# A hybrid encoder step on one core: the last projection as a software pipeline in program order, with blocks of 2, 2, 2, 2, 2, 1

## The chip, the cores and the metric

The kernel runs on one core of a Trainium2 chip. The metric is the device time of one execution in microseconds; the time before is the median of three runs. Engines are named as in the profile: PE (matrix multiply), PEld (its weight loads), DVE (vector), ACT (scalar), POOL (GpSimd), SP (the queue that issues most DMAs).

## The reference, cut to what matters

One layer of a streaming encoder. Three mixers read one normalised input; their outputs go through one output projection and are added to the residual stream. Then follows the gated feed-forward block, whose last product is what the change is about:

```python
x = x + jnp.concatenate([o_a, o_b, o_c], axis=-1) @ w_out
h = _rms_norm(x, norm2_g)
x = x + (jax.nn.silu(h @ w_gate) * (h @ w_up)) @ w_down
```

There are 1024 prompt rows and 64 sample rows (1088 together), a model width of 1024 and a hidden width of 2816. Everything is float32.

## The kernel before, in words

**Precision.** Each float32 operand is split into a high part (rounded by ACT, `acopy`) and a low part (the rest, a DVE subtraction, `tt`). A product is three matmuls: high x high, high x low, low x high.

**Gate and up.** The hidden width is cut into 11 stripes of 256 (`kp`), and each has a gate unit and an up unit: 22 units `u`. Each unit is a 2 x 2 block product by a seven-product scheme (Winograd's form of Strassen's), for two column halves `c` of the rows (`NB` = 256 and 288 wide). So a unit has 14 steps of 12 matmuls; units 0 and 21 run the seven steps of `c` = 0 and then those of `c` = 1, the others alternate. The results of an up unit are multiplied into `gate[c, i, j]`, and the generator `hidden(kp, c)` forms the seven left operands that the down stage needs, splits them (ACT and DVE, through tiles `e` and `ds`) and writes them to `hd` in DRAM; the sample's rows go to `hs`. `hidden` runs in small pieces, one at each step of a later unit; that of the last unit runs inside the down stage.

**Down.** The 11 stripes are worked off in blocks, `KB`. For each block there are four pairs of row tiles (`PAIRS`), and each pair has seven products (`STEPS`). Each product is 3 matmuls per stripe into a bank Y, Z or X. After each product DVE adds the bank to a row tile (`y_add` into `yf`), and later products of the pair add onto the same bank: Y takes products 0, 2, 4 and 6, Z takes 1 and 5, X takes 3. So product 2 may only start when the accumulation after product 0 has read Y, and so on. The sample's rows need two steps more in each block (8 matmuls per stripe in all). In the last block an output goes out by `y_out` (a DMA on SP) after each of the products 3, 4, 5 and 6 of a pair.

**Weights of down.** For each stripe `d_prep` loads four blocks of 128 x 512 (DMAs from POOL's queue), forms the differences T1 to T4 on POOL (`G.tensor_tensor`), and splits eight blocks (ACT rounds, DVE subtracts). They live in slots of 128 x 512 (`DS`). The left operands `a` are loaded from `hd` by `a_load` (SP) into a ring of nine tiles; `fetch` loads the next wanted one at each step.

**What sets the order.** The lists `work` and `plans` give the order in which the code names the operations, and a planner with a cost model orders each engine's queue from it. In the down loop `prep(b + 1)` takes one piece of the next block's plan after each step where enough slots are free, and the rest at the block's end. A queue runs in order: an instruction that waits holds up all behind it on its engine.

Of the kernel before, what the change touches and what calls it, by code (L numbers as in the profile page):

```python
# [7 lines left out]
F32 = mybir.dt.float32  # L8
# [7 lines left out]

EPS = 1e-6
# [35 lines left out]
def hybrid_step(ctx, tc, x_prompt, x_sample, cache_k, cache_v, st_gdn, st_conv, norm1_g, w_in, conv_w, a_log,  # L53
# [1397 lines left out]
    ev, _ev = pool("ffne", "right")  # L1451
    xb, _xb = pool("hT1", "right")
    xb_.append(xb)
    later = []
# [116 lines left out]
    hid = []  # L1571
    xs1 = x_sums(1)
    w_loads(1)
    for u in range(22):
        sa, sb_ = unit_steps(u, 0), unit_steps(u, 1)
        steps = sa + sb_ if u in (0, 21) else [s for p in zip(sa, sb_) for s in p]
        for i, s in enumerate(steps):
            s()
            flush()
            for q in hid[:1] if u < 21 else ():  # L1580
                if next(q, 1):
                    hid.remove(q)
            if u == 0 and i < 7:
                next(xs1, None)
            if i >= 7 or u not in (0, 21):
                n = i - 7 if u in (0, 21) else i // 2
                if u in (0, 21) or i % 2:
                    WS.give(*WA[u].pop(PRODUCTS[n][0]))
            if i == 7 - (u > 0) and u + 1 < 22:
                w_sums(u + 1)  # L1590
            if i >= 7 and u + 1 < 22:
                for n in ([i - 8] if 7 < i else []) + ([6] if i == 13 else []) if u == 0 else [i - 7]:
                    w_split(u + 1, PRODUCTS[n][0])
        WA.pop(u)
        if u + 2 < 22:
            w_loads(u + 2)


    _xb.close()
    _fl.close()  # L1600
    _xr.close()
    _xa.close()
    dp, _dp = pool("ffnd", "left")
    KB = ((0, 1), (2, 3, 4), (5, 6), (7, 8), (9, 10))
# [3 lines left out]
    D = {}  # L1608
    yf = {}
    lasts = {}  # L1610

    def y_tile(t):
        yf[t] = sb(dp, [128, DM], "yf%d" % t)

    def y_load(t):
        r = 64 if t == 8 else 128
        SP.dma_start(out=yf[t][:r], in_=yd[128 * t:128 * t + r, :])

    def a_tile():
# [12 lines left out]

    def d_prep(kp):


        L = D[kp] = {}

        def load():
            for i in range(2):
                for j in range(2):  # L1640
                    n = "B%d%d" % (i + 1, j + 1)
                    L[n] = DS.take()
                    f0 = 256 * kp + 128 * i
                    G.dma_start(out=L[n], in_=w_down[0, f0:f0 + 128, 512 * j:512 * j + 512])  # L1644

        def minus(n, a, b):
            L[n] = DS.take()
            G.tensor_tensor(out=L[n], in0=L[a], in1=L[b], op=ALU.subtract)  # L1648

        def sums(*args):  # L1650
            for q in args:
                minus(*q)

        def split(n):
            v, h, lo = L[n], DS.take(F32R), DS.take(F32R)
            lasts["A"] = acopy(h, v)
            lasts["V"] = tt(lo, v, h.bitcast(F32), ALU.subtract)
            L[n] = (h, lo)
            DS.give(v)
# [5 lines left out]
    def d_plan(kps):  # L1665
        heads, splits = zip(*[d_prep(kp) for kp in kps])
        plan = [h[0] for h in heads]
        if kps == KB[0]:
            plan += [x for y in zip(*heads) for x in y][len(kps):] + [x for y in zip(*splits) for x in y]
        else:  # L1670
            for h, x in zip(heads, splits):
                plan += h[1:] + x
        return plan

    AL = {}

    def a_load(key):
        b, p, n = key
        kps = KB[b]
        c, q = PAIRS[p][:2]  # L1680
        v = head if key == (0, 0, 0) else a_tile()
        SP.dma_start(out=v[:, :2 * len(kps)].bitcast(F32), in_=hd[n, 2 * c + q, :, 2 * kps[0]:2 * kps[-1] + 2, :])
        AL[key] = v

    def s_load(b):
        kps = KB[b]
        v = sb(dp, [128, 6, 128], "sm", F32R, bufs=2)
        SP.dma_start(out=v[:, :2 * len(kps)].bitcast(F32),
                     in_=hs[2 * kps[0]:2 * kps[-1] + 2].rearrange("f p t -> p f t"))
        AL[b] = v  # L1690

    def y_add(t, h, ps, b):
        c = slice(512 * h, 512 * h + 512)
        tt(yf[t][:, c], ps, yf[t][:, c], ALU.add)
# [10 lines left out]
    def pair_steps(b, p):  # L1705
        kps, banks = KB[b], {}

        def step(n, bank, adds):
# [5 lines left out]
            for k, kp in enumerate(kps):  # L1714
                bh, bl = D[kp][RIGHT[n]]
                if p == 3:
                    D[kp].pop(RIGHT[n])
                    DS.give(bh, bl)
                for l, r in ((a[:, 2 * k], bh), (a[:, 2 * k], bl), (a[:, 2 * k + 1], bh)):
                    T.matmul(ps, l, r, start=fresh and m == 0, stop=m == 3 * len(kps) - 1,  # L1720
                             skip_group_check=not fresh)
                    m += 1

            def add():
                for i, j, done in adds:
                    t = PAIRS[p][2 + i]
                    y_add(t, j, ps, b)
# [6 lines left out]
    def sample_steps(b):  # L1734
        kps = KB[b]

        def step(j):
            ps, v = mmb(), AL[b]
            m, last = 0, 4 * len(kps) - 1
            for k, kp in enumerate(kps):  # L1740
                for i in range(2):
                    B = D[kp]["B%d%d" % (i + 1, j + 1)]
                    for w in B:
                        mm(ps, v[:, 2 * k + i], w, m == 0, m == last)
                        m += 1
                    if (i, j) == (0, 1):
                        DS.give(*B)

            def add():
                slot = DS.take()  # L1750
                tmp = slot[:64]
# [4 lines left out]
                DS.give(slot)  # L1756
# [7 lines left out]
    for b in range(len(KB)):  # L1764
        order = ["s", 0, 1, 2, 3] if b else [0, "s", 1, 2, 3]
        for p in order:
# [8 lines left out]
    def fetch():  # L1775
        if wants:
# [3 lines left out]
    plans = [d_plan(kps) for kps in KB]  # L1780

    def prep(b, n=1, room=6):

        while n and b < len(KB) and plans[b] and len(DS.free) >= plans[b][0][0] + room:
            plans[b].pop(0)[1]()
            n -= 1

    fetch()
    prep(0, 2)
    fetch()  # L1790
    fetch()
    for t in PAIRS[0][2:]:
        y_load(t)
    for _ in range(3):
        fetch()
    prep(0, 6)
    y_tile(8)
    y_load(8)
    for p in PAIRS[1:]:
        for t in p[2:]:  # L1800
            y_tile(t)
    prep(0, 10, 0)
    fetch()
    fetch()
    for i, (b, p, n, f) in enumerate(work):
        if b == 0 and p == 0:
            prep(0, 2, 0)
            if n in (1, 4):
                y_load(PAIRS[1][2 + n // 4])
        if b == 0 and p in (1, 2) and n in (1, 4):  # L1810
            y_load(PAIRS[p + 1][2 + n // 4])
        if p == "s":
            prep(b, 99, 0)
# [3 lines left out]
        if hid and i > 4:  # L1817
            with tc.issue_after(lasts["A"].ins), tc.issue_after(lasts["V"].ins):
                if next(hid[0], 1):
                    hid.pop(0)  # L1820
            if not hid:
                _ev.close()
                dq, _dq = pool("ffne2", "right")
                DS.more(dq, "f", 16)
# [36 lines left out]
```

## Time and profile before

| | |
|---|---|
| time before, median of 3 runs | 1377.42 us (1375.39 to 1378.45) |
| the profiled execution: time | 1375.35 us |
| its span, first to last instruction | 1373.6 us |
| mean granted clock of PE | 0.986 |
| PE busy | 1324.0 us (96%) |
| DVE busy | 989.2 us (72%) |
| ACT busy | 678.7 us (49%) |
| POOL busy | 185.5 us (14%) |

All times of the profile count from the start of the span. A row of a group reads: line, engine, operation, what it writes and from what, shape, count, then busy time and mean duration in ns, then idle time of the engine just before and what ended it. A row of the busy times by stretch reads: stretch, its length, then for PE, PEld, DVE, ACT and POOL the busy time with the count of instructions, then the granted clock of PE (1.00 is full), the share of the DMA engines and GB/s. A row of the chain of waits or of the timeline begins with the start and the duration in us. In a row of DMA issues the last number is the median time from issue to landing. Most small operations are recorded at the line of a helper: L85 is `acopy`, L91 is `tt`, L94 is `mm`; L1464 is the gate/up product, L1720 the down product, L1644 and L1648 the load and the difference in `d_prep`, L1682 `a_load`, L1699 `y_out`.

### The profile page before, as it was taken

Reading aid. Unit: us, or ns where it says so; the run is one execution under the profiler, and the core shown is the slowest. Engines: PE = TensorE matmul, PEld = TensorE weight load, DVE = VectorE, ACT = ScalarE, POOL = GpSimd, SP = SyncE. Lnnn points to the kernel's source line nnn. Section 1 sums busy time; section 2 is a strip of 40 time slices with the busy share of each in tenths; the row PEclk is TensorE's granted clock in tenths of the full one; section 3 lists DMA queues with packets and bytes.
Section 4 is the critical chain, followed back from the end, with each engine's and each line's share of the span. In section 5 each row is a group of like instructions: output and inputs, shape, how many; then the busy total and the mean of one; then the engine's idle time right before and its main releaser. Section 6 shows DMA issues by size and latency. Waiting matters only on the chain.

```text
span 1373.6 us, 26500 instructions
## 1 busy us (share of the span) xinstructions
PE 1324.0 (96%) x9922; PEld 1179.7 (86%) x9922; DVE 989.2 (72%) x2296; ACT 678.7 (49%) x1733; POOL 185.5 (14%) x274
## 2 busy tenths in 40 slices
PE   6999999999999999999999999999999988998898
PEld 6988888888878877778999999999999966776687
DVE  5887877867788775498776677666776498566854
ACT  7677376674566654557544555445554333121200
POOL 3100130101222200200000000000000435151400
PEclk9999999999999999998999999999999989999999
DMA  8432332223333262221443454434544689665566
GB/s 258 118 80 60 97 99 78 78 63 79 83 93 93 62 216 65 101 71 53 153 125 114 152 173 137 124 119 141 174 151 123 214 283 325 190 196 172 180 180 233
DMA packets 201314, 188.99 MB, mean 138 GB/s; under 512 B 13819, under 2 KB 170464, under 8 KB 201186
## 3 DMA queue, kind: packets, MB, share of 16 engines
q1 hardware_dynamic: 196018, 171.43, 41.4%
q0 software_dynamic: 5008, 15.77, 3.4%
q8 instruction: 78, 1.28, 0.4%
q14 instruction: 50, 0.41, 0.1%
q10 hardware_dynamic: 160, 0.10, 0.0%
HBM read 135.72 MB, written 51.61 MB: 136 GB/s over the span
## 4 chain that ended last, share of the span: by engine, by line
PE 84%; DVE 7%; DMA 3%; issue 2%; ACT 2%; POOL 1%; SPq 0%; DVEq 0%; ACTq 0%; POOLq 0%
PE ax L1464 29%; PE mm L94 26%; PE ax L1720 10%; PE ax L94 10%; PE mm L1464 5%; DVE d L91 2%; PE mm L1720 2%; DVE yf L91 1%; DMA d<-in_ffn_w_down_dram 1%; PE ax L502 1%; PE ax L274 1%; DVE lw L91 1%; PE ax L837 1%; DVE f L91 1%; DMA xs<-in_x_prompt_dram 0%
## 5 line engine op out<-in xcount | busy, mean ns | idle before, releaser
L1464 PE MATMUL ax<-x,w 128*128 128x256 f32 (+1 forms) x2552 | 359.3, 288 | 0.0
L1464 PEld LDWEIGHTS ax<-x,w 128*128 128x128 f32 x2552 | 335.4, 191 | 0.2
L91 DVE TENSOR_TENSOR w<-w,w 128x512 fp32r<-128x512 f32 (+1 forms) x242 | 164.5, 688 | 87.8 <-PE ax L1464 51.3
L1720 PE MATMUL ax<-d,a 128*128 128x512 f32 x644 | 176.5, 406 | 19.1 <-DVE yf L91 15.5
L1720 PEld LDWEIGHTS ax<-d,a 128*128 128x128 f32 x644 | 124.9, 195 | 52.0 <-DVE yf L91 19.7
L94 PE MATMUL mm<-xh,hw 128*128 128x384 f32 (+1 forms) x432 | 151.3, 350 | 0.0
L94 PE MATMUL mm<-xl,hw 128*128 128x384 f32 (+1 forms) x432 | 143.6, 332 | 0.0
L94 PE MATMUL mm<-xh,lw 128*128 128x384 f32 (+1 forms) x432 | 143.2, 331 | 0.0
L85 ACT ACTIVATE hw<-wr 128x512 fp32r<-128x512 f32 (+2 forms) x168 | 99.7, 619 | 65.6 <-PE mm L94 55.1
L91 DVE TENSOR_TENSOR lw<-wr,hw 128x512 fp32r<-128x512 f32 (+2 forms) x168 | 110.8, 674 | 25.0 <-ACT hw L85 24.3
L91 DVE TENSOR_TENSOR yf<-ax,yf 128x512 f32<-128x512 f32 x120 | 82.2, 687 | 61.4 <-PE ax L1720 58.3
L1464 PE MATMUL ax<-xr,w 128*128 128x288 f32 x616 | 116.0, 296 | 0.0
L85 ACT ACTIVATE w<-w 128x512 fp32r<-128x512 f32 x154 | 94.5, 623 | 29.1 <-PE mm L1464 15.2
L85 ACT ACTIVATE s<-ax 128x256 f32<-128x256 f32 (+1 forms) x132 | 52.0, 394 | 87.8 <-PE ax L1464 87.5
L1464 PEld LDWEIGHTS ax<-xr,w 128*128 128x128 f32 x616 | 95.0, 188 | 0.2 <-ACT s L85 0.2
L94 PEld LDWEIGHTS mm<-xh,hw 128*128 128x128 f32 x432 | 81.1, 188 | 10.2 <-issue 7.3
L1644 POOL DMA_DIRECT2D d<-in_ffn_w_down_dram x37 | 19.8, 541 | 479.6 <-PE ax L1464 455.8
L94 PEld LDWEIGHTS mm<-xl,hw 128*128 128x128 f32 x432 | 81.4, 189 | 1.3 <-issue 0.7
L94 PEld LDWEIGHTS mm<-xh,lw 128*128 128x128 f32 x432 | 81.1, 188 | 1.2 <-issue 0.3
L85 ACT ACTIVATE d<-d 128x512 fp32r<-128x512 f32 x58 | 33.6, 622 | 75.2 <-POOL d L1648 47.9
L1464 PE MATMUL mm<-x,w 128*128 128x256 f32 (+1 forms) x528 | 70.6, 289 | 0.0
L88 DVE SCALAR_TENSOR_TENSOR tr<-tr,cw 128x384 f32<-128x384 f32 (+1 forms) x108 | 64.1, 594 | 7.2 <-ACT tr L85 6.2
(337 smaller groups left out, 2518.2 us busy)
## 6 DMA issues: line engine op xcount, KB each, us to landing
hd<-e SPq DMA_DIRECT2D x154, 256.0 KB, 2.4
wr<-in_w_in_dram SPq DMA_DIRECT2D x72, 512.0 KB, 3.9
a<-hd SPq DMA_DIRECT2D x112, 256.0 KB, 3.2
w<-in_ffn_w_gate_dram SPq DMA_DIRECT2D x44, 256.0 KB, 3.4
w<-in_ffn_w_up_dram SPq DMA_DIRECT2D x44, 256.0 KB, 3.5
a<-hd SPq DMA_DIRECT2D x28, 384.0 KB, 3.2
d<-in_ffn_w_down_dram POOLq DMA_DIRECT2D x37, 256.0 KB, 6.0
wr<-in_w_out_dram SPq DMA_DIRECT2D x9, 512.0 KB, 4.4
```

The costliest lines, as they stand in the source:

```text
L85: return A.activation(out=out, in_=in_, func=AF.Copy, scale=scale)
L88: return V.scalar_tensor_tensor(out=out, in0=in0, scalar=s, in1=in1, op0=op0, op1=op1)
L91: return V.tensor_tensor(out=out, in0=in0, in1=in1, op=op)
L94: return T.matmul(out, lhsT, rhs, start=start, stop=stop)
L274: T.transpose(b[k // 4][:, (k % 4) * r:(k % 4) * r + r], x[:r, k * 128:k * 128 + 128], ident[:r, :r])
L502: T.transpose(b[u // 4][:, (u % 4) * 128:(u % 4) * 128 + 128], src(u).rearrange("p h i -> p (h i)"), ident)
L837: T.transpose(PTp[0:r0 + cnt, j, kv, :], P[:, kv, 128 * j:128 * j + r0 + cnt], ident)
L1464: T.matmul(ps[:, :NB[c]], a[:, k, :], b[:, k, :], start=first and i == 0, stop=i == 11, skip_group_check=not first)
L1644: G.dma_start(out=L[n], in_=w_down[0, f0:f0 + 128, 512 * j:512 * j + 512])
L1720: T.matmul(ps, l, r, start=fresh and m == 0, stop=m == 3 * len(kps) - 1, skip_group_check=not fresh)
```

## The change

From unit 21 to the end the planner is switched off: on all five engines the instructions run in the order in which the code names them. The preparation of each block's weights is written out as a table of steps (`ORDER0` for block 0, within unit 21; `ORDER` for a later block, within the block before it). The blocks are (0,1), (2,3), (4,5), (6,7), (8,9), (10) where they were (0,1), (2,3,4), (5,6), (7,8), (9,10).

The weights are loaded as two rows of blocks per stripe, each 128 x 1024 (R1, R2), from SP's queue and no longer from POOL's. ACT and DVE split R1 and R2 in single operations of 1024; the differences are rounded and subtracted in pairs of 512 (T13, T24). The slots for them (`PT`) come from the places of the gate/up stage's right operands as each is used up (`left_over`): 15 and then 19, 2 more from `yf` places, and 8 where `hidden`'s tiles were, once `hidden` has ended. The differences, the tiles `a` and the sample's temporary share the 20 slots `w` of the gate/up weights (`WS`). `fetch` no longer uses a ring of nine but holds back when `AL` has nine entries. Within a step of the down loop the order is: the matmuls, the accumulation (and `y_out`), `fetch`, a load of `yf`, one piece of `hidden` on every second step, and up to three pieces of the next block's plan.

The diff, cut to its core:

```diff
+ENGINES = {getattr(mybir.EngineType, n) for n in ("PE", "DVE", "Activation", "Pool", "SP")}
...
+    KB = ((0, 1), (2, 3), (4, 5), (6, 7), (8, 9), (10,))
...
+        def load(i):
+            L["R%d" % (i + 1)] = t = PT.take()
+            f0 = 256 * kp + 128 * i
+            SP.dma_start(out=t.rearrange("p j c -> p (j c)"), in_=w_down[0, f0:f0 + 128, :])
...
+            G.tensor_tensor(out=block(t), in0=a, in1=b, op=ALU.subtract)
...
+        def rnd(n):
+            h = PT.take(F32R)
+            L[n, "h"] = h
+            if n[0] == "R":
+                acopy(h, L[n])
+            else:
+                for j in range(2):
+                    acopy(h[:, j], block(L["T" + n[1 + j]]))
+
+        def sub(n):
+            h, lo = L[n, "h"], PT.take(F32R)
+            L[n, "l"] = lo
+            if n[0] == "R":
+                tt(lo, L[n], h.bitcast(F32), ALU.subtract)
+                used(n)
...
+                for j in range(2):
+                    tt(lo[:, j], block(L[names[j]]), h[:, j].bitcast(F32), ALU.subtract)
+                    WS.give(L[names[j]])
...
+    ORDER0 = ((0, "aL1 aL2"), (1, "bL1 bL2"), (5, "aT1d aR1r"), (6, "bT1d aR1s bR1r"), (7, "aT3d bR1s"),
+              (8, "bT3d aR2r"), (9, "aT2d aT13r aR2s"), (10, "bT2d aT13s bT13r"), (11, "aT4d bT13s bR2r"),
+              (12, "bT4d aT24r bR2s"), (13, "aT24s bT24r"), (14, "bT24s"))
+    ORDER = ((0, "aL1 aL2"), (8, "aT1d aR1r"), (9, "aT3d"), (10, "aT2d aR1s"), (11, "aT4d aR2r"),
+             (12, "bL1 bL2 aT13r"), (13, "aR2s"), (14, "aT13s aT24r"), (16, "aT24s"), (19, "bT1d"), (20, "bT3d bR1r"),
+             (21, "bT2d"), (22, "bT4d bR1s bR2r"), (24, "bR2s bT13r"), (26, "bT13s bT24r"), (28, "bT24s"))
...
+    def prep(b, t, most=3):
+
+        while most and b < len(KB) and plans[b] and plans[b][0][0] <= t and len(PT.free) >= plans[b][0][1]:
+            plans[b].pop(0)[2]()
+            most -= 1
...
+    def s_load(b):
+        kps = KB[b]
+        AL[b] = v = WS.take(F32R)
...
+            ps, a = banks[bank], AL.pop((b, p, n))
...
+                for i, j, done in adds:
+                    t = PAIRS[p][2 + i]
+                    y_add(t, j, ps)
+                    if done and b + 1 == len(KB):
+                        y_out(t, j)
...
+        def step(j):
+            ps, v = mmb(), AL[b]
...
+    def fetch():
+        if wants and len(AL) < 9:
+            k = wants.pop(0)
+            s_load(k) if isinstance(k, int) else a_load(k)
...
     for u in range(22):
+        if u == 21:
+            ctx.enter_context(tc.manual_schedule(engines=ENGINES))
...
+            if u == 21:
+                left_over(i)
+                prep(0, i, 4)
+                if i > 7:
+                    fetch()
...
+    for i, (b, p, n, f) in enumerate(work):
+        if i and b > work[i - 1][0]:
+            start = i
+            prep(b, 99, 99)
+        f()
+        flush()
+        fetch()
+        if b == 0 and p in (0, 1) and n in (2, 5):
+            y_load(PAIRS[p + 2][2 + n // 5])
+        if hid and i > 1 and i % 2 == 0:
+            if next(hid[0], 1):
+                hid.pop(0)
+            if not hid:
+                _ev.close()
+                dq, _dq = pool("ffne2", "right")
+                PT.add(dq, "f", 8, 8)
+        prep(b + 1, i - start)
...
-    KB = ((0, 1), (2, 3, 4), (5, 6), (7, 8), (9, 10))
...
-                    G.dma_start(out=L[n], in_=w_down[0, f0:f0 + 128, 512 * j:512 * j + 512])
...
-        return ([(4, load), (2, lambda: sums(("T1", "B12", "B11"), ("T2", "B22", "T1"))),
-                 (2, lambda: sums(("T3", "B22", "B12"), ("T4", "B21", "T2")))],
-                [(2, lambda n=n: split(n)) for n in ("B11", "T1", "T2", "B21", "T3", "B22", "T4", "B12")])
...
-        if not (b == 0 and p in (0, "s")):
-            prep(b + 1)
-        if i + 1 < len(work) and work[i + 1][0] > b:
-            prep(b + 1, 99, 0)
```

In the tables `a` and `b` are the two stripes of a block, L1 and L2 their loads, T..d a difference on POOL, ..r a rounding on ACT, ..s a subtraction on DVE; the number is the step from which it may stand.

More of the change, by code (lines that the diff above doesn't have):

```diff
@@ new lines, in hybrid_step @@
+    work = []
+    for b in range(len(KB)):
+        for p in (["s", 0, 1, 2, 3] if b else [0, "s", 1, 2, 3]):
+            work += [(b, p, None, f) for f in sample_steps(b)] if p == "s" else \
+                    [(b, p, x[0], f) for x, f in zip(STEPS, pair_steps(b, p))]
+    wants = []
+    for b, p, n, f in work:
+        k = b if p == "s" else (b, p, n)
+        if k not in wants:
+            wants.append(k)
+    def fetch():
+        if wants and len(AL) < 9:
+            k = wants.pop(0)
+            s_load(k) if isinstance(k, int) else a_load(k)
@@ L1685, in s_load @@
[L1685 to L1694, printed above, removed]
-    def y_out(t, h):
-        c = slice(512 * h, 512 * h + 512)
-        dst = y_p[0, 128 * t:128 * t + 128, c] if t < 8 else y_s[0, :, c]
-        SP.dma_start(out=dst, in_=yf[t][:dst.shape[0], c])
@@ L1702, in hybrid_step @@
-    STEPS = ((0, "Y", ((0, 0, 0),)), (1, "Z", ((1, 1, 0),)), (2, "Y", ((0, 1, 0),)), (3, "X", ((0, 0, 1),)),
-             (4, "Y", ((1, 1, 1),)), (5, "Z", ((0, 1, 1),)), (6, "Y", ((1, 0, 1),)))
-    def pair_steps(b, p):
-        kps, banks = KB[b], {}
-        def step(n, bank, adds):
-            fresh = bank not in banks
-            if fresh:
-                banks[bank] = mmb() if bank == "X" else ax()
-            ps, a = banks[bank], AL.pop((b, p, n))
-            m = 0
[L1714 to L1727, printed above, removed]
-                    if done and b + 1 == len(KB):
-                        y_out(t, j)
-            later.append(add)
-        return [lambda x=x: step(*x) for x in STEPS]
@@ L1734, in sample_steps @@
[L1734 to L1751, printed above, removed]
-                c = slice(512 * j, 512 * j + 512)
-                acopy(tmp, ps[64:128, :])
-                tt(yf[8][:64, c], ps[0:64, :], yf[8][:64, c], ALU.add)
-                tt(yf[8][:64, c], tmp, yf[8][:64, c], ALU.add)
-                DS.give(slot)
-                if b + 1 == len(KB):
-                    y_out(8, j)
-            later.append(add)
-        return [lambda j=j: step(j) for j in range(2)]
@@ L1780, in hybrid_step @@
[L1780 to L1813, printed above, removed]
-        f()
-        flush()
-        fetch()
[L1817 to L1824, printed above, removed]
-        if not (b == 0 and p in (0, "s")):
-            prep(b + 1)
-        if i + 1 < len(work) and work[i + 1][0] > b:
-            prep(b + 1, 99, 0)
```

215 lines of the change are left out of this document (138 added, 77 removed).

## The prediction

> **What bounds the kernel now.** I read the page first: the span, the busy shares, the granted clock.
>
> ```profile
> span 1373.6 us, 26500 instructions
> PE 1324.0 (96%) x9922; PEld 1179.7 (86%) x9922; DVE 989.2 (72%) x2296; ACT 678.7 (49%) x1733; POOL 185.5 (14%) x274
> ```
>
> PE bounds the program, but the change touches only its last fifth. So next come the busy times by stretch, cut where PE stops being full; the fields are length, then busy time and instructions of PE, weight loads, DVE, ACT, POOL, then granted clock.
>
> ```profile
> 1074.80:1096.00 21.20, 21.20 (x170) 21.20 (x169) 6.54 (x13) 4.59 (x10) 12.89 (x15) 1.00 0.74 240
> 1096.00:1120.00 24.00, 17.72 (x53) 13.32 (x52) 22.91 (x33) 9.61 (x22) 13.08 (x18) 0.72 0.83 283
> 1120.00:1180.00 60.00, 50.96 (x205) 39.41 (x205) 51.46 (x83) 23.39 (x45) 22.70 (x21) 0.94 0.89 291
> 1180.00:1220.00 40.00, 40.00 (x175) 32.56 (x174) 16.51 (x22) 3.39 (x7) 6.08 (x5) 1.00 0.63 179
> 1220.00:1250.00 30.00, 22.81 (x89) 17.59 (x88) 27.15 (x36) 11.19 (x20) 17.20 (x15) 0.89 0.51 153
> 1270.00:1300.00 30.00, 25.90 (x110) 19.96 (x109) 25.64 (x36) 10.20 (x18) 14.26 (x13) 1.00 0.57 176
> 1300.00:1369.60 69.60, 69.60 (x303) 56.30 (x301) 35.49 (x52) 1.19 (x2) 0.00 (x0) 1.00 0.69 211
> ```
>
> The last gate/up unit (u = 21: 14 steps of 12 matmuls) fills 1074.8 to 1096.0 with DVE at 31% and ACT at 22%. The down stage runs from 1096.0 to 1369.6. The chain of waits gives its pace where nothing disturbs it:
>
> ```profile
> 1355.80 8.28 PE ax L1720 x36
> 1364.07 1.39 PE mm L1720 x6
> 1369.63 0.69 DVE yf L91
> ```
>
> One pair of seven products is 42 matmuls in 9.67 us, 0.230 us each. The code issues per 256 weight rows 4 pairs x 7 products x 3 and 8 for the sample, 92; times 11 is 1012, so PE needs 233.0 us, the same before and after. The stage takes 273.6, so 40.6 us are lost. By counts against 0.230: 11.8 in 1096-1120, 12.8 in 1120-1180, 9.5 in 1220-1250, 4.7 in 1270-1300. These are the stretches in which DVE is 86 to 95% busy. The list of waits, from 1050 on, says so:
>
> ```profile
> PE ax L1720 <- DVE yf L91: 20.6, 11, 3.5
> ```
>
> PE waits for DVE's accumulation into `yf`, which stands in DVE's queue behind bunches of weight subtractions. That is what the change spreads out.
>
> **The change part by part.** The groups of DVE and POOL from 1096 on, and ACT's from the page:
>
> ```profile
> L91 DVE TENSOR_TENSOR yf<-ax,yf 128x512 f32<-128x512 f32 x120 | 82.2, 687 | 61.4 <-PE ax L1720 58.3 <-DMA yf<-yd 2.6
> L91 DVE TENSOR_TENSOR d<-d,d 128x512 fp32r<-128x512 f32 x49 | 39.3, 840 | 1.8 <-ACT d L85 1.8
> L91 DVE TENSOR_TENSOR e<-g,e 128x256 fp32r<-128x256 f32 x10 | 4.4, 444 | 1.3 <-ACT e L85 1.3
> L1648 POOL TENSOR_TENSOR d<-d,d 128x512 f32<-128x512 f32 x18 | 27.3, 1530 | 11.2 <-DVE yf L91 6.0 <-PE ax L1720 3.2 <-DMA d<-in_ffn_w_down_dram 1.2
> L85 ACT ACTIVATE d<-d 128x512 fp32r<-128x512 f32 x58 | 33.6, 622 | 75.2 <-POOL d L1648 47.9
> ```
>
> When DVE has a backlog, 512-wide operations follow each other at 0.60 us (chain of waits):
>
> ```profile
> 1240.32 0.60 DVE d L91
> 1240.92 1.21 DVE yf L91 x2
> ```
>
> *Loads.* 44 loads of 256 KB leave POOL (44 x 0.54 = 24 us of a mostly idle engine, worth nothing on the path) and 22 of 512 KB go to SP. The nearest rows bound the landing at 3.2 and 4.4 us:
>
> ```profile
> a<-hd SPq DMA_DIRECT2D x112, 256.0 KB, 3.2
> d<-in_ffn_w_down_dram POOLq DMA_DIRECT2D x37, 256.0 KB, 6.0
> wr<-in_w_out_dram SPq DMA_DIRECT2D x9, 512.0 KB, 4.4
> ```
>
> I take 4.4 (same size and queue). Block 0's four go out by step 1 of u = 21 (1077.8), land by about 1083, and PE needs them at 1096: nothing, with 13 us of cover; without it, 4.4.
>
> *Block 0's preparation inside u = 21* is what can be gained at the start. ACT has 8 roundings of 1024 (8 x 1.24) in steps 5 to 13: it fits. DVE in order has 8 subtractions of 1024, at most 2 x 0.60 each, among the combines. The combine of step 10 starts at 1091.5; from there DVE owes seven combine operations (about 3.0) and five subtractions (5.9), so the last (`bT24s`) ends near 1100.4, and the first accumulation, queued behind it, near 1101.1. Product 2 writes the bank that this accumulation reads, and would start at 1098.8: PE loses 2.4.
>
> *Block 0 itself.* DVE still owes the last unit's `hidden` (about 9 us: 22 operations of 256 at 0.44 or less), 28 accumulations, 2.7 for the sample, 9.3 for block 1's subtractions: some 40 us against 42.5 of PE. Walking the order: `hidden` takes every second step up to 16, bL2 has no slot until `hidden` is done at step 16, and three subtractions then come in steps 16 and 17. An accumulation may be late by 0.7 us (the spare of a 1.38 us step); behind steps 8, 10 and 17 it is later, and PE waits 0.6, 0.8 and 2.8: 4.2. DVE beside POOL is the unknown:
>
> ```profile
> 1109.20 4.10 DVE L91 TENSOR_TENSOR ds<-g 128x256 f32<-128x256 f32 x1
> 1109.28 3.73 POOL L1648 TENSOR_TENSOR d<-d,d 128x512 f32<-128x512 f32 x3
> ```
>
> A 0.42 us operation lasted 4.10 beside three of POOL's. Bounds for the sixteen POOL subtractions near u = 21 and block 0: none hit, 0; all sixteen block for 1.53, 24. The mean subtraction of the stage, 840 ns, is 0.24 over its 0.60, so I am near the low end: 16 x 0.16 = 2.5. With 1 us for a clock drop, the start and block 0 cost 10.1 (bounds 6 to 32).
>
> *Blocks 1 to 4.* A block's 28 accumulations, sample and 8 subtractions are about 32 us of DVE in 42.5, one subtraction at a time, so a late accumulation mostly stays inside its 0.7 us. I take 3 in all (0 to 6) where before 14.2 were lost in 1220-1250 and 1270-1300.
>
> *One more block* adds 28 accumulations and 4 sample adds, about 22 us of DVE, and 29 loads of 0.32 on SP. They hide in the slack, except in block 5, where a product is 3 matmuls, 0.69, no more than its accumulation.
>
> *The last block's queue order* is what the change adds. `fetch` holds back at nine entries in `AL`, and the sample tiles are never taken out of `AL`: in block 5 six of nine are such, and only three products are loaded ahead (nine before). SP issues in program order, and each `y_out` waits for its accumulation. SP before, in its last stretch:
>
> ```profile
> 1355.83 0.32 SPq L1682 DMA_DIRECT2D a<-hd  x1
> 1356.55 0.34 SPq L1699 DMA_DIRECT2D out_dram<-yf  x1
> 1358.15 12.54 SPq L1699 DMA_DIRECT2D out_dram<-yf  x7
> ```
> ```profile
> SPq L1699 <- DVE yf L91: 16.4, 17, 5.1
> ```
>
> So `y_out` really stops SP (17 times). Now the load of product n + 3 stands right behind the `y_out` of product n, for n = 3 to 6. Landing of `a`, before and after stores join it (1331-1338, 1338-1345):
>
> ```profile
> L1682 SPq DMA_DIRECT2D a<-hd x5: 319/320/412, 1332.3 to 1337.9; - x5
> DMA to landing us min/median/max: 2.7/2.9/3.0
> ```
> ```profile
> DMA to landing us min/median/max: 3.8/3.8/3.9
> ```
>
> The new tiles are half as large; I take 2.9 (2.4 to 3.8). From the end of product 3: accumulation 0.03 + 0.69, store issue 0.03 + 0.34, landing 2.9, wake-up 0.1 = 4.09, while products 4 and 5 last 1.38: PE idles 2.71 before product 6. The same comes before product 2 of the next pair, behind the `y_out` of product 6. That is 4 + 3 gaps, 19.0. At the block's start the sample's stores hold product 3's load in the same way: DVE ends the sample's four adds 1.85 after the second sample product, + 0.03 + 0.34 + 2.9 + 0.1 = 5.2 against 2.1 us of products 0 to 2: 3.1. Sum 22.1 (18.6 to 28.8 by the landing).
>
> *Sum.* 1096.0 + 233.0 + 10.1 + 3 + 22.1 + 4.0 (from PE's end to the end of the span, as now: 1373.6 - 1369.6) = 1368.2, 5.4 less than 1373.6. The profiled execution took 1375.35, 2.07 under the median of 1377.42; I move by the same amount, to 1372.0.
>
> *Clock.* Gaps of 2.7 us are where the clock may drop. Two PE rows with their gap, and the stretches after:
>
> ```profile
> 1113.95 2.50 PE L1720 MATMUL ax<-d,a 128*128 128x512 f32 x5 [2.73 <-DVE yf L91]
> 1172.73 0.50 PE L1720 MATMUL ax<-d,a 128*128 128x512 f32 x1 [2.96 <-DVE yf L91]
> ```
> ```profile
> 1114.00:1116.00 2.00, 2.00 (x5) 1.62 (x6) 1.83 (x5) 0.05 (x1) 0.00 (x0) 0.50 1.03 404
> 1172.00:1174.00 2.00, 1.27 (x6) 1.05 (x7) 0.93 (x3) 1.72 (x4) 1.21 (x1) 1.00 0.39 144
> ```
>
> One gap of 2.73 left the clock at half, one of 2.96 did not. At half, a product of the last block takes 1.28; walking a pair as above gives 12.0 us instead of 10.25, so 7.0 more. The Trainium skill ("TensorE: Matmul & The Clock Gate", section "Why this matters for your kernels") puts the limit at gaps of about 3 us; by that rule the last block stays at full clock and the sum is as above, but the row at 1113.95 speaks against it.
>
> **The rivals.**
> A. *Half clock through the last block*: 1372.0 + 7.0 = 1379.0. For it the gap at 1113.95, and seven gaps in 40 us; against it the one at 1172.73.
> B. *The stores don't hold SP in effect* (loads run far enough ahead, or land in time): the last block loses only 3 by the accumulation chain, 1372.0 - 19.1 = 1352.9. Against it: 16.4 us of SP's waits on exactly these stores; for it: the 20 `w` slots would allow more than three tiles ahead.
> C. *Slower, by one mechanism: POOL blocks DVE in u = 21 and block 0.* There DVE has no slack, and each block of 1.53 goes straight to PE. The row of 4.10 speaks for it, the mean of 840 ns against it. All sixteen: 2.5 becomes 24, 1393; ten: 1385. It decides from 8.2 us more, about seven of the sixteen. The Trainium skill ("SBUF — State Buffer", section "Who interferes with whom") says that a DVE instruction with two SBUF inputs and a GpSimd instruction that reads SBUF exclude each other for a whole instruction; the trace agrees in that one row.
>
> **How the numbers follow.** 0.2% (2.75 us) is about what this measurement can tell from no change. My case 0.42 (1372.0, own range 1365 to 1379: of it 0.30 faster, 0.10 same, 0.02 slower), A 0.20 (0.04, 0.10, 0.06), B 0.18 (all faster), C 0.20 (0.02 same, 0.18 slower). Faster 0.52, same 0.22, slower 0.26. The range runs from B's 1353 to C's ten blocks, 1385.
>
> **What would show it.** PE at 0.230 per matmul at full clock without gaps over 1 us in blocks 1 to 4; a gap of 2 to 3 us at the third product of the down stage, led by DVE; in the last 45 us about seven gaps near 2.7, released by landings of `a`, with SP's `y_out` waiting on DVE just before. I am wrong if the last block has no such gaps (B), if its clock is 0.5 (A), or if DVE's subtractions before 1140 last over 2 us (C).

## The result, and the profile after

The changed kernel takes 1391.15 us, the median of four runs (1390.07 to 1394.69), beside 1376.72 for the kernel before on the same chip: a ratio of 1.0109, 95% interval 1.0086 to 1.0131. It is slower by 1.1%; 1372.0 had been predicted, with a range up to 1385. The profiled execution has this span and these busy times:

```profile
span 1389.8 us, 26486 instructions
PE 1326.8 (95%) x9922; PEld 1176.0 (85%) x9922; DVE 999.0 (72%) x2306; ACT 676.7 (49%) x1713; POOL 163.3 (12%) x230
```

PE's work is the same 9922 matmuls: of the 16.2 us by which the span grew, 13.4 are idle time of PE, and 2.8 are longer busy time for the same work. The busy times by stretch of the changed kernel, in the columns used before, say where:

```profile
1096.00:1120.00 24.00, 18.52 (x86) 14.78 (x84) 20.33 (x35) 4.64 (x11) 5.72 (x4) 1.00 0.89 308
1120.00:1180.00 60.00, 42.97 (x174) 33.45 (x175) 39.48 (x61) 17.38 (x33) 12.36 (x8) 0.89 0.80 260
1220.00:1250.00 30.00, 29.65 (x128) 23.54 (x127) 22.13 (x30) 4.32 (x6) 5.37 (x4) 1.00 0.52 164
1270.00:1300.00 30.00, 29.96 (x130) 23.70 (x129) 23.98 (x33) 3.85 (x6) 8.04 (x7) 1.00 0.50 162
1339.80:1386.00 46.20, 30.33 (x93) 19.02 (x91) 21.83 (x32) 1.19 (x2) 0.00 (x0) 0.85 0.52 162
```

The middle is what the change set out to make: PE is busy for 29.65 and 29.96 of 30 us in the two stretches where the kernel before had 22.81 and 25.90. The ends are worse: 42.97 of 60 us (50.96 before) in 1120-1180, and 30.33 of 46.2 us in the last block, where the kernel before ran its last 69.6 us without a gap. The list of waits of PE from 1050 on names DVE's accumulations first and landings of the left operands second:

```profile
PE ax L1721 <- DVE x L92: 20.0, 7, 12.3
PE ax L1721 <- DMA w<-hd: 12.4, 10, 2.3
PE ax L1721 <- issue: 4.2, 2, 2.5
```

(In this trace the row tiles `yf` carry the name `x`, the left operands `a` the name `w`, and the weights `x`, `xr` or `f`, after the pools their places come from. L86 is `acopy`, L92 `tt`, L95 `mm`; L1721 is the down product, L1682 `a_load`, L1703 `y_out`, L1627 a difference on POOL.)

I cut the stage at the first sample matmul of each later block, with which that block begins. The first of block 1 and of block 5:

```profile
1165.91 0.39 PE L95 MATMUL mm<-xr,w 128*128 128x512 f32 x1
...
1339.77 0.39 PE L95 MATMUL mm<-f,w 128*128 128x512 f32 x1
```

At 0.230 us a matmul, the start and block 0 (184 matmuls, 42.4 us) should take PE from 1096.0 to 1138.4; block 1 begins at 1165.9, so **27.5 us** are lost there. PE is idle for 22.4 of them: 0.93 before the last step of unit 21, and 21.5 from the stage's first product on. About 3 go because matmuls after the gaps run at a lower clock. And 1.9 were lost before the part that the change is about, since unit 21 began later in this execution than in the one profiled before (first row: before; second: changed; the variants below lie between 1074.9 and 1076.4):

```profile
1074.80 4.47 PE L1464 MATMUL ax<-x,w 128*128 128x256 f32 x36
```
```profile
1076.66 4.48 PE L1465 MATMUL ax<-x,w 128*128 128x256 f32 x36
```

Blocks 1 to 4 take 173.9 for 169.5: **4.4** lost. Block 5 takes 46.2 for 21.4: **24.8** lost. The kernel before lost 24.6 in 1096-1180, 14.2 in the middle and next to nothing at the end. So the middle gained 9.8 us, the last block lost some 24, and the start, where 14.5 were to be gained, lost 2.9 more.

**The last block.** Its PE rows with a gap over 1.8 us, and SP's rows around one of them:

```profile
1351.97 0.77 PE L1721 MATMUL ax<-x,w 128*128 128x512 f32 x1 [2.26 <-DMA w<-hd]
1363.67 0.47 PE L1721 MATMUL ax<-x,w 128*128 128x512 f32 x1 [2.24 <-DMA w<-hd]
1374.29 0.47 PE L1721 MATMUL ax<-x,w 128*128 128x512 f32 x1 [1.97 <-DMA w<-hd]
1385.11 0.47 PE L1721 MATMUL ax<-x,w 128*128 128x512 f32 x1 [2.24 <-DMA w<-hd]
```
```profile
1354.77 1.82 SPq L1682 DMA_DIRECT2D w<-hd  x4
1360.43 0.34 SPq L1703 DMA_DIRECT2D out_dram<-x  x1
1360.86 0.38 SPq L1682 DMA_DIRECT2D w<-hd  x1
```

SP issues four loads by 1356.6, then nothing until the store of 1360.43, whose accumulation has just ended; the load behind it, issued at 1360.86, lands just before PE resumes at 1363.67. A pair comes round every 11.0 us ((1385.11 - 1351.97) / 3), for 4.8 of PE at full clock.

**Block 0.** The chain of waits through it has DMA landings of `hidden`'s stores where one would look for engines:

```profile
1114.10 5.82 DMA hd<-e
1120.02 0.43 ACT e L86
...
1125.99 6.55 DMA hd<-e
1132.64 0.42 ACT e L86
1133.09 0.43 DVE e L92
1133.54 4.78 DMA hd<-e
1138.43 0.42 ACT e L86
1138.88 0.44 DVE e L92
1139.33 2.60 DMA hd<-e
...
1144.39 5.09 DVE f L92 x3
1149.48 0.61 DVE x L92
1150.13 2.07 PE ax L1721 x4
```

`hidden` goes through a ring of three tiles `e`. A rounding into a tile must wait until the store that read it has landed, and DVE, in program order, waits behind the rounding. ACT's list of waits for 1099-1154 sums it up, and DVE's, POOL's and PE's rows show how it reaches PE:

```profile
ACT e L86 <- DMA hd<-e: 16.9, 6, 8.9
```
```profile
1138.88 0.42 DVE L92 TENSOR_TENSOR e<-g,e 128x256 fp32r<-128x256 f32 x1 [0.23 <-ACT e L86]
1142.05 1.22 DVE L92 TENSOR_TENSOR f<-xr,x 128x1024 fp32r<-128x1024 f32 x1 [2.75 <-DMA hd<-e]
1143.19 0.68 DVE L92 TENSOR_TENSOR x<-ax,x 128x512 f32<-128x512 f32 x1
1143.79 5.69 DVE L92 TENSOR_TENSOR f<-w,f 128x512 fp32r<-128x512 f32 x4
1149.40 0.68 DVE L92 TENSOR_TENSOR x<-ax,x 128x512 f32<-128x512 f32 x1
```
```profile
1143.83 1.77 POOL L1627 TENSOR_TENSOR w<-f,x 128x512 f32<-128x512 f32 x1 [8.00 <-DMA w<-hd]
1145.56 3.38 POOL L1627 TENSOR_TENSOR w<-f,w 128x512 f32<-128x512 f32 x2
```
```profile
1150.13 2.07 PE L1721 MATMUL ax<-x,w 128*128 128x512 f32 x4 [12.31 <-DVE x L92]
```

The 12.31 us in which PE idles add up along these rows, from 1137.82: 1.48 to the end of `hidden`'s last subtraction, 2.75 in which DVE stands before a weight subtraction whose slot `f` lies over `hidden`'s old tiles, still being read by its stores; 1.14 for that subtraction; 0.60 for one accumulation; 5.61 for four subtractions beside POOL; 0.73 for the accumulation that PE waits for and the start of the matmul. In this order the accumulations stand behind weights that PE needs some 15 us later.

### The profile page after: what moved, and what is told of

The parts are those of the page before. It is cut to its first block, busy times and chain, and to the rows that moved or that the text cites. A ratio compares the mean times of both kernels' runs of the same rounds, so it can differ in the third digit from the quotient of the medians.

```text
span 1389.8 us, 26486 instructions
## 1 busy us (share of the span) xinstructions
PE 1326.8 (95%) x9922; PEld 1176.0 (85%) x9922; DVE 999.0 (72%) x2306; ACT 676.7 (49%) x1713; POOL 163.3 (12%) x230
## 3 DMA queue, kind: packets, MB, share of 16 engines
q8 instruction: 78, 1.28, 0.4%
## 4 chain that ended last, share of the span: by engine, by line
PE 84%; DVE 7%; DMA 5%; ACT 2%; issue 2%; POOL 1%; SPq 0%; DVEq 0%; ACTq 0%; POOLq 0%
PE ax L1465 29%; PE mm L95 26%; PE ax L1721 10%; PE ax L95 10%; PE mm L1465 5%; DVE x L92 3%; PE mm L1721 2%; DMA w<-hd 2%; DMA hd<-e 1%; PE ax L503 1%; PE ax L275 1%; DVE lw L92 1%; PE ax L838 1%; DMA xs<-in_x_prompt_dram 0%; DVE tr L89 0%
## 5 line engine op out<-in xcount | busy, mean ns | idle before, releaser
L1465 PEld LDWEIGHTS ax<-x,w 128*128 128x128 f32 x2552 | 336.5, 191 | 0.2
L92 DVE TENSOR_TENSOR w<-w,w 128x512 fp32r<-128x512 f32 (+1 forms) x242 | 164.1, 687 | 88.9 <-PE ax L1465 51.1
L1721 PE MATMUL ax<-x,w 128*128 128x512 f32 x476 | 147.8, 407 | 34.1 <-DVE x L92 19.6
L95 PE MATMUL mm<-xh,hw 128*128 128x384 f32 (+1 forms) x432 | 151.3, 350 | 0.0
L1721 PEld LDWEIGHTS ax<-x,w 128*128 128x128 f32 x476 | 92.1, 194 | 62.9 <-DVE x L92 26.6
L92 DVE TENSOR_TENSOR x<-ax,x 128x512 f32<-128x512 f32 x144 | 97.9, 687 | 65.3 <-PE ax L1721 65.1
L95 PE MATMUL mm<-xl,hw 128*128 128x384 f32 (+1 forms) x432 | 143.5, 332 | 0.0
L95 PE MATMUL mm<-xh,lw 128*128 128x384 f32 (+1 forms) x432 | 143.2, 331 | 0.0
L86 ACT ACTIVATE hw<-wr 128x512 fp32r<-128x512 f32 (+2 forms) x168 | 99.7, 619 | 65.7 <-PE mm L95 55.0
L92 DVE TENSOR_TENSOR lw<-wr,hw 128x512 fp32r<-128x512 f32 (+2 forms) x168 | 110.7, 673 | 25.0 <-ACT hw L86 24.3
L86 ACT ACTIVATE w<-w 128x512 fp32r<-128x512 f32 x154 | 94.5, 624 | 29.8 <-PE mm L1465 15.2
L86 ACT ACTIVATE s<-ax 128x256 f32<-128x256 f32 (+1 forms) x132 | 52.1, 395 | 85.5 <-PE ax L1465 85.1
L95 PEld LDWEIGHTS mm<-xh,hw 128*128 128x128 f32 x432 | 81.1, 188 | 10.1 <-issue 7.3
L95 PEld LDWEIGHTS mm<-xl,hw 128*128 128x128 f32 x432 | 81.4, 188 | 1.3 <-issue 0.7
L95 PEld LDWEIGHTS mm<-xh,lw 128*128 128x128 f32 x432 | 81.1, 188 | 1.2 <-issue 0.3
L1627 POOL TENSOR_TENSOR w<-x 128x512 f32<-128x512 f32 x9 | 12.4, 1380 | 548.3 <-PE ax L1465 447.3
L1721 PE MATMUL ax<-f,w 128*128 128x512 f32 x200 | 70.9, 413 | 2.9 <-DMA w<-hd 2.3
L86 ACT ACTIVATE e<-g 128x256 fp32r<-128x256 f32 x110 | 45.6, 414 | 50.5 <-DMA hd<-e 26.6
```

The costliest lines, as they stand in the source:

```text
L86: return A.activation(out=out, in_=in_, func=AF.Copy, scale=scale)
L92: return V.tensor_tensor(out=out, in0=in0, in1=in1, op=op)
L95: return T.matmul(out, lhsT, rhs, start=start, stop=stop)
L1465: T.matmul(ps[:, :NB[c]], a[:, k, :], b[:, k, :], start=first and i == 0, stop=i == 11, skip_group_check=not first)
L1627: G.tensor_tensor(out=block(t), in0=a, in1=b, op=ALU.subtract)
```

## The experiments

All are edits of the changed kernel. Where two numbers are compared across groups of runs, the ratio to the kernel before is the safer one. The table has, from each profile, the start of block 1, what the start and block 0 lost (as above), the length of block 0 from its own first product, which leaves out when unit 21 began, the part of it in which PE is idle, and the length of block 5 (21.4 of work). The work of block 0 is 42.4 us; what its length exceeds work and idle time together is matmuls at a lower clock.

| kernel | time, us | ratio to before, 95% | block 1 starts | lost up to there | block 0 | of it PE idle | block 5 |
|---|---|---|---|---|---|---|---|
| changed | 1391.15 | 1.0109 (1.0086-1.0131) | 1165.9 | 27.5 | 66.8 | 21.5 | 46.2 |
| e1_pop | 1370.63 | 0.9957 (0.9945-0.9969) | 1164.5 | 26.1 | 66.0 | 18.4 | 29.3 |
| e2_yact | 1374.78 | 0.9977 (0.9964-0.9991) | 1165.8 | 27.4 | 67.9 | 19.0 | 30.8 |
| e3_ering | 1385.94 | 1.0068 (1.0045-1.0091) | 1157.2 | 18.8 | 59.2 | 10.5 | 49.9 |
| e4_hact | 1398.71 | 1.0161 (1.0139-1.0184) | 1169.4 | 31.0 | 72.1 | 20.5 | 48.9 |
| e5_popring | 1362.94 | 0.9901 (0.9883-0.9919) | 1155.2 | 16.8 | 56.7 | 10.6 | 27.4 |
| e6_late | 1360.37 | 0.9876 (0.9851-0.9900) | 1153.6 | 15.2 | 56.0 | 8.3 | 27.7 |
| e7_fast | 1357.43 | 0.9855 (0.9834-0.9876) | 1150.3 | 11.9 | 51.5 | 5.9 | 27.7 |
| e8_fdelay (one run) | 1362.93 | - | 1154.7 | 16.3 | 57.2 | 10.5 | 28.4 |
| e9_delayonly | 1385.93 | 1.0058 (1.0041-1.0074) | 1161.3 | 22.9 | 62.7 | 11.8 | 49.0 |
| e10_fastlate | 1356.06 | 0.9842 (0.9825-0.9858) | 1148.9 | 10.5 | 50.3 | 5.7 | 27.4 |

**e1_pop: the last block's loads run further ahead.** The sample's tiles are taken out of `AL` once used, so `fetch` may again hold nine products.

```diff
             if j:
                 WS.give(v)
+                AL.pop(b)
```

> One line: the sample tile is taken out of AL after its second use, so fetch may hold nine products again in every block. Theory (three products ahead, each load behind a store that waits): the last block, 46.0 us in the changed kernel against 21.2 of matmuls, falls to about 25, all gaps behind landings of a go; 1391 becomes about 1371. Rival (the stores' traffic makes the loads land late, or accumulation sets the pace of a block of one stripe): the gaps stay, time within 5 us of 1391. Blocks 0 to 4 as in the changed kernel for both.

Measured: 1370.63 us. The last block in one stretch, the same work as above:

```profile
1338.80:1368.10 29.30, 26.18 (x93) 17.14 (x91) 21.81 (x32) 1.19 (x2) 0.00 (x0) 0.94 0.68 217
```

It falls from 46.2 to 29.3 us; block 0 keeps its gap (12.25). One line is worth 20 us of time, 16.9 of them visible in this block. So the depth of the loads ahead of the stores makes most of the last block's loss.

**e2_yact: the same place, mended in another way.** The output stores are issued from ACT's queue; the loads stay three products deep.

```diff
-        SP.dma_start(out=dst, in_=yf[t][:dst.shape[0], c])
+        A.dma_start(out=dst, in_=yf[t][:dst.shape[0], c])
```

> y_out is issued from ACT's queue instead of SP's; the nine entries of AL stay as they are, so still only three products ahead in the order of the code. Theory (SP is held by the stores' waits): SP runs ahead as far as the free w slots allow and the last block's gaps go, about 1371, as if the depth had been mended. Rival 1 (three ahead is too few whatever the queue does): the gaps stay, about 1391. Rival 2 (the stores' traffic): the stores move as many bytes at the same times, the gaps stay, about 1391.

Measured: 1374.78 us, block 5 30.8. The same stores move the same bytes. The code still names each load only three products ahead, but SP, no longer held, has issued all 28 of the block's loads by 1354.5, when PE is in its ninth product of 28:

```profile
1321.46 33.03 SPq L1682 DMA_DIRECT2D w<-hd  x28
```

So it was the store's wait in SP's order that kept the loads close to PE, and not the stores' traffic. How little depth would do is not shown, since SP ran further ahead here than three products.

**e3_ering: `hidden` of the last unit without its ring of three.** Its tiles `e` come from the 20 slots `w`.

```diff
-        e = sb(ev, [128, 2, 2, 128], "e", F32R, bufs=3)
+        w = WS.take(F32R) if kp == 10 else None
+        e = w.rearrange("p (q h) t -> p q h t", q=2) if w is not None else sb(ev, [128, 2, 2, 128], "e", F32R, bufs=3)
...
+        if w is not None:
+            WS.give(w)
```

> hidden's tile e for the last stripe comes from the free w slots (8 to 12 in block 0) instead of the ring of three. Theory (in block 0 DVE stands in order behind hidden, which waits for its ring of three to land in DRAM): the gaps of 3.6 and 2.6 us go and the gap of 12.3 shrinks to 5 to 8 (three subtractions beside POOL remain), time about 1379. Rival 1 (POOL's exclusion of DVE sets block 0): no more than 3 us. Rival 2 (hidden's stores stand on SP behind loads that wait for slots): the ring is only a symptom; with more tiles DVE no longer waits for it, but the f slots still wait for the stores, 4 to 8 us.

Measured: 1385.94 us. Of the gaps in block 0 the one of 2.59 goes, as expected, and the one of 12.31 becomes 3.69 (5 to 8 expected), but the one near 1120 stays (4.22). Block 1 begins 8.7 us earlier, 1.1 of it because unit 21 began earlier; block 0 itself is 7.6 shorter. The time falls by only 5.2, because the last block grows by 3.7. Its stretch shows why:

```profile
1331.30:1381.20 49.90, 35.98 (x93) 22.54 (x91) 21.84 (x32) 1.19 (x2) 0.00 (x0) 0.72 0.49 150
```

The 93 matmuls take 35.98 us and not 30.33, at a granted clock of 0.72 and not 0.85. The gaps are the same or smaller (2.07 at most).

**e4_hact: `hidden`'s stores from ACT's queue**, so that they don't stand behind waiting loads on SP.

```diff
-        SP.dma_start(out=hd[n, 2 * c:2 * c + 2, :, 2 * kp:2 * kp + 2].rearrange("q p h t -> p q (h t)"),
+        (A if kp == 10 else SP).dma_start(out=hd[n, 2 * c:2 * c + 2, :, 2 * kp:2 * kp + 2].rearrange("q p h t -> p q (h t)"),
```

> The seven hd stores of each half of the last stripe are issued from ACT's queue instead of SP's; the ring of three stays. Rival 2 of the run before (the stores stand on SP behind weight loads that wait for slots): the ring turns as fast as a landing allows and 8 to 12 us go, about 1381. Theory of the ring alone (landing, 2 to 3 us for three tiles): 2 to 5 us go, since only the queueing on SP goes. If POOL sets block 0: nothing changes.

Measured: 1398.71 us, slower, which no theory had. ACT's list of waits for 1099-1154:

```profile
ACT e L86 <- DVE e L92: 24.6, 6, 15.0
ACT e L86 <- DMA hd<-e: 10.2, 4, 5.2
```

The wait for landings does fall, from 16.9 to 10.2. But the store waits for DVE's subtraction and now stands in ACT's order ahead of the next rounding, which DVE needs: waits of 24.6 us. The longest of them, 15.0, stands about where the changed kernel waited 9.6 and 5.3 for DVE's first pieces of `hidden`; the rest is new. A waiting store takes its wait to the queue that it moves to; in e2 ACT had almost nothing left to hold up (two instructions in the last block). But this is not what makes e4 slower than the changed kernel. PE is idle for 20.5 us of block 0, 1.0 less than there, and the block is 5.2 longer because its matmuls take longer: the granted clock is 0.70 in 1120-1160 against 0.83, and in the last block 0.76 against 0.85. Why it is lower is not shown.

**e5_popring: e1 and e3 together.**

> Both edits together: the sample tile leaves AL, and hidden's tile e of the last stripe comes from the w slots. If the two losses are separate (last block on SP, block 0 on DVE), the gains add: 1370.6 less the 7.5 us by which block 0 was shorter with the second edit, 1363; the last block as in the first edit (29 us), block 0 from its first product to block 1's first sample product 59. If the second gain came only because loads and stores moved on SP, less than 3 us remain, 1368 or more.

Measured: 1362.94 us. The two losses add, and with the last block's gaps gone the clock there (1.00) no longer takes back what block 0 gains. Two gaps of 4.1 and 4.0 us remain in block 0; the next two kernels ask what they are.

**e6_late: e5 with POOL's differences for block 1 named after `hidden`** (from step 16 of block 0, not from 8), by a table of its own for that block:

```diff
+    ORDER1 = ((0, "aL1 aL2"), (8, "aR1r"), (10, "aR1s"), (11, "aR2r"), (16, "aT1d aR2s"), (17, "aT3d aT2d bL1"),
...
-        plans.append([(t,) + ops[x[0]][x[1:]] for t, names in (ORDER if n else ORDER0) for x in names.split()
+        plans.append([(t,) + ops[x[0]][x[1:]] for t, names in (ORDER if n > 1 else ORDER1 if n else ORDER0) for x in names.split()
```

> As the run before, and POOL's eight differences for block 1 stand after hidden (steps 16 to 24 instead of 8 to 22), with DVE's subtractions ordered to suit. Theory (what is left in block 0 is POOL excluding DVE while hidden runs): hidden's 256-wide subtractions fall from a mean of 0.74 us to 0.45, the gap of 4.2 us goes, 3 to 6 us faster than the run before, 1358. Rival (DVE is simply full in block 0): the same work, crowded into fewer steps, waits at steps 17 to 28 instead, within 2 us of the run before or slower.

Measured: 1360.37 us, 2.6 less than e5, between the two theories and with overlapping intervals; block 0 from its first product is 0.7 shorter. The first gap fell from 4.09 to 1.76, the second stayed (3.77). `hidden`'s subtractions did not get shorter in the mean (500 ns in e5, 528 here, those of the form `w<-g,w`), but the long rows changed places. In e5 three DVE rows ahead of the first gap's accumulation are long, while POOL works beside them:

```profile
1114.26 1.72 DVE L92 TENSOR_TENSOR x<-w,x 64x512 f32<-64x512 f32 x1
1117.66 1.37 DVE L92 TENSOR_TENSOR g<-g,ds 128x256 f32<-128x256 f32 x1
1118.95 1.49 DVE L92 TENSOR_TENSOR w<-ds,w 128x256 fp32r<-128x256 f32 x1
```

The same three take 0.68, 0.43 and 0.42 in e6, where POOL stands still until 1131. Then it works beside `hidden`'s last pieces, ahead of the second gap:

```profile
1131.33 1.51 DVE L92 TENSOR_TENSOR w<-ds,w 128x256 fp32r<-128x256 f32 x1
1132.76 1.51 DVE L92 TENSOR_TENSOR w<-g,w 128x256 fp32r<-128x256 f32 x1
```

So POOL beside DVE did stretch the first gap, by about 2.3 us, and this edit moved the delay to a later place more than it removed it.

**e7_fast: e5 with a piece of `hidden` at every step**, not every second, so that it ends by step 10 and its slots come free well before step 16.

```diff
-        if hid and i > 1 and i % 2 == 0:
+        if hid and i > 1:
```

> As e5, but hidden runs a piece on every step from 2 on, so it ends at step 9 and its slots come free seven steps earlier. If block 0 is limited by DVE's sum of work, nothing changes (1363). If the late slots are what crowds steps 16 and 17 (the gap of 3.7 us there), that gap goes and PE waits more before step 9: 1 to 4 us faster. If DVE's bunching is what counts (hidden pieces of 1.1 us against 0.7 us of spare per step), 3 us slower.

Measured: 1357.43 us, 1.5% faster than the kernel before. The second gap is gone. PE's rows with a gap, from 1096 to block 1:

```profile
1097.11 1.86 PE L1465 MATMUL ax<-xr,w 128*128 128x288 f32 x12 [0.93 <-DVE s L92]
1104.22 0.47 PE L1724 MATMUL ax<-x,w 128*128 128x512 f32 x1 [2.49 <-issue]
1120.85 0.80 PE L1724 MATMUL ax<-x,w 128*128 128x512 f32 x1 [3.19 <-DVE x L92]
1136.32 3.24 PE L1724 MATMUL ax<-x,w 128*128 128x512 f32 x13 [0.26 <-DVE x L92]
```

**e8_fdelay and e9_delayonly: which wait makes the 12.3 us?** The ring of three stays, and the eight slots `f` over `hidden`'s tiles are handed out at step 20; e8 does this on top of e1, e9 alone.

```diff
-                PT.add(dq, "f", 8, 8)
+        if i == 20:
+            PT.add(dq, "f", 8, 8)
```

> As e1 with the ring of three, but the f slots (in the place of hidden's tiles) are handed out at step 20 instead of 16, when hidden's stores have landed. Theory (in the gap of 12.3 us DVE and ACT stand in order behind f slots that wait for landings): no wait of DVE for a store of hd before an f tile, the gap falls to 3 to 8 us, 1365 to 1369; the block's last steps are more crowded. Rival (the ring alone makes the gap): the gap stays over 10 us, 1371 or more.

> The changed kernel with one edit: the eight slots over hidden's old tiles are handed out at step 20 of block 0 and not as soon as hidden's code has ended at step 16; the loads of the last block are held back as in the changed kernel. Theory (block 0's loss is mostly DVE and ACT standing in order behind slots that wait for hidden's stores to land): the 12.3 us gap of PE goes and block 1 starts 9 to 10 us earlier, near 1156, as it did together with the deeper loads (1154.7 against 1164.5). The last block stays a run of gaps near 2 us, and as in the run with the larger ring a part may be given back there to half clock: 1381 to 1387. Rival (the landing of the e ring, not the slots): the gap stays over 10 us and the time within 2 us of the changed kernel's 1391.

Measured: 1362.93 us for e8 (one run) and 1385.93 for e9. In both the long gap is gone: the longest gap of block 0 after that of product 2 is 2.26 in e8 and 3.78 in e9, with the ring of three in place and ACT still waiting for landings (13.9 and 21.6 us in 1099-1154). So the ring alone does not make the long gap; it takes the slots `f` in DVE's and ACT's order, with the accumulations behind them. The delay also moves the subtractions into `f` behind some accumulations; what they cost at step 16 without the ring's waits is read from e3 and e5, where 3.69 and 4.03 of the long gap remain. The same four subtractions, in e8, and POOL's first difference after them:

```profile
1142.44 2.49 DVE L92 TENSOR_TENSOR f<-w,f 128x512 fp32r<-128x512 f32 x4
```
```profile
1145.22 1.27 POOL L1627 TENSOR_TENSOR w<-f,x 128x512 f32<-128x512 f32 x1 [11.27 <-DMA f<-in_ffn_w_down_dram]
```

2.49 us without POOL, 5.69 beside it (4.68 beside it in e9). In e9 PE is idle for 9.7 us less of block 0, so the wait itself is worth what was expected of it. But block 1 begins only 4.6 us earlier, not 9 to 10, and the stretch of 40 us shows what took the rest:

```profile
1120.00:1160.00 40.00, 31.74 (x109) 24.46 (x110) 28.71 (x47) 12.06 (x24) 6.06 (x4) 0.83 0.86 277
```

109 matmuls took 31.74 us, 6.6 more than at 0.230: half clock after gaps of 2.79, 3.78 and 2.23. That step of my expectation failed; which gaps lower the clock I could not foretell.

**e10_fastlate: e7 with e6's table.**

> The fastest kernel so far (sample tiles taken out of AL, e from the larger pool, hidden a piece at every step: 1357.4) with one more edit: POOL's differences for block 1 come from step 16 on, after hidden, and not from step 8. Theory: what block 0 still loses there is the gap of 3.2 us and late accumulations; if POOL beside hidden's DVE work makes it, it goes and the time is 1354 to 1355. Rival (slots crowded into steps 16 and 17 are what costs): in this kernel hidden has ended by step 10, the later table crowds the subtractions again into steps 17 to 20, and the time is the same or up to 3 us longer, 1357 to 1360.

Measured: 1356.06 us; block 1 begins 1.4 us earlier than in e7, and the gap of 3.19 is 2.69. The intervals of the two overlap, so they cannot be told apart by time. With `hidden` at this pace, what POOL beside it costs is about 1.2 us of block 0 (51.5 against 50.3), as far as one profile of each can tell.

**The gap near 1120**, of 1.8 to 5.1 us in all the variants, is the wait for one accumulation, that after the first product of the second pair. It stands in DVE's order behind the sample's four adds and four subtractions of `hidden` (more in e7 and e10). The gap is 1.75 or 1.76 where nothing stretches these (e1, e6, e8), 3.60 in the changed kernel, where DVE stood idle 1.68 and 0.28 among them for roundings that waited for landings, and 4.09 in e5, where the three rows above are long.

## Why the prediction was wrong, step by step

**The step that failed: the start and block 0.** The sum had 10.1 us, measured 27.5: 17.4 of the 21.6 us by which the span exceeds the sum (1389.8 against 1368.2); 1.9 of the 17.4 are the later start of unit 21. The prediction priced `hidden` as 9 us of DVE's busy time and set its end at step 16. It left out that each of its roundings needs a tile whose store has landed, that in strict program order such a wait holds all of ACT's and DVE's later work, and that the slots freed by `hidden` are not free until its stores have landed. The landing of these stores was 3.0 us (median) in 1096-1160 before and is 4.5 in 1096-1155 after, the longest 7.9. The term also had 1 us for the clock, and about 3 went there. With the ring's waits taken out it is still 16.8 (e5); only with `hidden` at a piece a step as well does it come near the sum's, to 11.9 in e7 and 10.5 in e10. The order there isn't the predicted one, and the waits lie elsewhere (3.19 near 1120 and 0.26 later, for 0.6, 0.8 and 2.8 behind steps 8, 10 and 17), so that agreement is in part luck. What I missed is the ring `e`, and its row stood in the trace of before, in ACT's list of waits for 1090-1200, where I had read DVE's and PE's:

```profile
ACT e L85 <- DMA hd<-e: 8.9, 7, 3.6
```

There the planner let DVE do other work in the meantime: DVE itself stood 1.3 us behind these roundings, and 7.6 in the changed kernel.

**The steps that held.** Product 2 of the stage idles 2.49 for 2.4 predicted (the row names no releaser, but the accumulation that it needs ends at 1104.38, just before). Both ends of that wait lie some 3 us later than in the sum: the stage begins at 1099.07 and not at 1096.0, and DVE's last subtraction ends at 1103.8 and not at 1100.4. The loads for block 0 cost nothing. Blocks 1 to 4 lose 4.4 (3 predicted, 0 to 6). One wait the sum did not have: a combine of unit 21 stands behind two subtractions (2.39 us together, beside POOL), and PE's last step there waits 0.93 for it.

**The last block: right in place and nearly in size, with another make-up.** 24.8 lost against 22.1. The chain was as described, a store that holds SP and a load behind it, and e1 and e2 show it from both sides. But of the seven gaps of 2.71 the four before product 6 are 2.0 to 2.3, and the three before product 2 of the next pair are each split into two short ones, 0.9 to 1.4 together; only the block's start is as predicted (3.25 for 3.1). All idle time is 15.9 us, and 8.9 more go because the matmuls take 30.33 us and not 21.4. That is rival A, half clock, for a part of the time: 11.0 us a pair, between the 10.25 of full clock and the 12.0 of half. At a slower clock PE hides more of the same landing, so the two errors nearly cancel: the size was right by luck. Rival B (the stores don't hold SP) falls: with the hold removed by e1 the same kernel is at 1370.6. (The bounds of 18.6 to 28.8 count the landing seven times and leave out the one at the block's start; by the prediction's own terms they are 18.1 to 29.3.)

**Rival C** named the right block and the right sign, but the wrong mechanism for most of the loss. Subtractions beside POOL do take longer (5.69 against 2.49 for four), 3.2 us of the 12.3; and three rows of 256 in block 0 take 1.40, 1.51 and 1.47 where 0.42 is their length alone, 3.1 more, not all of it on PE's path; the two subtractions at the end of unit 21 add 1.1 (2.39 for 1.28). So the 2.5 I took for POOL was short by up to 5 us, and not by the 8.2 at which that rival decides. (The term used 0.16 for each subtraction, the mean of 840 ns less the 0.68 that one takes, where the sentence ahead of it has 0.24; with 0.24 it is 3.8.) That rows beside POOL lengthen agrees with the rule of the Trainium skill that I quoted ("SBUF — State Buffer", "Who interferes with whom").

**The clock.** The rule quoted there from the Trainium skill ("TensorE: Matmul & The Clock Gate", "Why this matters for your kernels"), which asks for no idle gaps over about 3 us, is not enough here: in e3's last block no gap is longer than 2.07 and the clock is 0.72 over 50 us. Another section of that page, "A second HAM failure mode: psum-queue depth-cycling", says that frequent short idles can make the clock swing between half and full; the rows of e3 and of the changed kernel agree with that one.

The remaining difference is in my favour: I added 3.8 us from span to median, and 1.35 are found. So 17.4 + 1.4 + 2.7 - 0.2 (tail) - 2.45 makes 18.9 of the 19.2 us by which 1372.0 was missed.

**What stays open.** Why the clock is lower in block 0 of e4 than in the changed kernel, and why the last block is at 0.85 in the changed kernel and at 0.72 to 0.79 in e3, e4 and e9, with gaps of much the same length (at most 2.26, against 2.07, 2.38 and 2.68); and why `hidden`'s stores took longer to land than before.

## What to carry to other kernels

When a planner is replaced by program order, price every instruction twice: by how long it works, and by how long it may stand waiting with the others behind it; DMA stores are the ones to look at, since they keep a ring's tile, and the place it lies in, until they land. Never name a load behind a store that waits for the current product, and let a slot be handed out when its last reader is done, not when the code that used it has ended. A pipeline that is perfect in its middle is decided at its two ends: here the middle gave 9.8 us and the ends took 26 until a few small edits gave it back.

## What the runs showed of the hardware that I had not expected

- Half clock without any long gap: in e3's last block gaps of 0.35 to 2.07 us, PE busy for 72% of the time, and a granted clock of 0.72; the changed kernel with gaps to 2.26 was at 0.85.
- The landing of a 256 KB store grew from 3.0 to 4.5 us (median), with single ones at 7.9. The busy share of the DMA engines does not explain it: 0.85 of 1110-1140 after, and 0.92 before.
- Four 512-wide subtractions took 5.69 us beside three of POOL's and 2.49 us alone.
- Stores moved from SP's to ACT's queue made the kernel 1.3% faster in one place (e2: 0.9977 against 1.0109), where ACT had two instructions left. In another (e4) ACT's roundings waited 24.6 us for DVE, and the kernel was 0.5% slower (1.0161, intervals just apart), though by a lower clock and not by more idle time of PE.
